# Reading the moving weight columns of a hybrid encoder block from two halves in turn

## The chip, the core and the metric

The kernel runs on one core of a Trainium2 chip. The core has a matrix engine (TensorE, PE in the profile; its weight loads are shown apart as PEld), a vector engine (DVE), a scalar engine (ACT), GpSimd (POOL) and SyncE (SP), which here issues most transfers. All engines work on SBUF; a matmul writes to PSUM. A matmul has two operands: a stationary one of up to 128 x 128, loaded by LDWEIGHTS, and a moving one, whose columns stream past it. The metric is device microseconds for one execution of the whole program. Host work before the launch, such as arranging the weights, is not in it.

## What is computed

One layer of an encoder block for 256 tokens of width 2048: an input projection that feeds two branches (an mLSTM and a gated delta rule, both in two directions), a gated merge of the two, an output projection, and a SwiGLU feed-forward part of width 5632. Cut to the parts that matter here:

```python
h = rms_norm(x, norm_mix_w) * (1 + scale_m) + shift_m
proj = h @ w_in
...
y_a = (jax.nn.sigmoid(a_o.astype(f32)) * h_a).astype(x.dtype) @ w_branch_a
...
y_b = (o_b * jax.nn.silu(b_z.astype(f32))).astype(x.dtype) @ w_branch_b
g_a, g_b = jnp.split(jax.nn.sigmoid(merge), N_BRANCH, axis=-1)
x = x + gate_m * ((g_a * y_a + g_b * y_b) @ w_out)
hf = rms_norm(x, norm_ffn_w) * (1 + scale_f) + shift_f
gt, up = jnp.split(hf @ w_gate_up, 2, axis=-1)
x = x + gate_f * ((jax.nn.silu(gt) * up) @ w_down)
```

Everything is float32. The large products are each computed as three: an operand is split into a high part of type fp32r and the rest, and high x high, low x high and high x low are summed in PSUM.

## The kernel before

There are two kinds of large product. A **product by feature** (`fjob`, lines 173 to 193) gives 128 features for all 256 tokens: the weights are stationary, the activations move, 256 columns at a time (lines 187 to 189). A **product by token** (`tjob`, from line 195) gives 512 features for 128 tokens at a time: the activations are stationary (`xh` and `xl`, the high and the low part, 128 tokens of one block of 128 inputs), and the weights move, 512 columns at a time.

`tjob` gets its weights as chunks of 128 x 4 x 512, 1 MB each, one transfer on SP's queue for one chunk (line 206). ACT copies half a chunk into the high part `wh` (line 209), DVE subtracts that from the raw weights to get `wl` (line 211); both are 128 x 2 x 512. For each of the two blocks in them and each of the two groups of 128 tokens PE issues three products (lines 230 to 232): `xh` with `wh`, `xl` with `wh`, `xh` with `wl`. `wh[:, k]`, the moving operand, is 512 consecutive fp32 values in each partition. The results of both token groups gather in two banks of PSUM, over all inputs, before ACT or DVE takes them out.

These jobs carry the z gate (named `z` in the trace), the values and output gates of the mLSTM (`v`, `o`), both merge gates (`ma`, `mb`), the two branch projections (`ya`, `yb`), the output projection (`o` with `mgh` and `mgl`), the gate and up products of the feed-forward part (`gt`, `up`) and its down product (`d`). The last output projection and the last down product end `by_token`: their last chunk is worked through for one token group after the other, and for the output projection the second group in two pieces of 256 columns (lines 253 to 255).

The work of the two branches between the projections (convolutions, the triangular inverses at lines 684 to 700, scans, small fp32 products such as `ks` at line 630) is threaded between these jobs, so that PE runs a large product while the other engines prepare the next small step. The first stretch, up to about 138 us, is the first input projection in plain fp32 (line 557), while the modulation weights stream in.

On the host, `_groups` cuts a weight matrix into chunks of 512 inputs by 512 outputs, laid out so that a chunk is one contiguous transfer. The gate and up weights are laid out the same way by a reshape of their own (`gu`).

Of the kernel before, what the change touches and what calls it, by code (L numbers as in the profile page):

```python
# [15 lines left out]
P = 128  # L16
# [36 lines left out]
def hybrid_block(ctx: ExitStack, tc: tile.TileContext, xr, nfr, crow, pk_d, cst_d, ada2, ada4, win0, winb, wint, wba, wbb, wo, wgu, wd, out, dbg=None):  # L53
    nc = tc.nc
    V, S, G, PE = nc.vector, nc.scalar, nc.gpsimd, nc.tensor
# [15 lines left out]
    def order(ins, yes=True):  # L71

        return tc.keep_in_program_order(ins) if yes else ins
# [62 lines left out]
    def raw_tile(shape, name):  # L136

        since[0] += 1
        if since[0] > 2 and asked and room[0][0] is st:
            add()  # L140
        return st.tile(shape, F32, tag="raw", bufs=3, name=name)
# [4 lines left out]
    def settle(keep=0, only=None):  # L146

        now = [f for f in behind if only is None or f.__name__ == only]
        for f in now[: len(now) - keep]:
            behind.remove(f)  # L150
            f()
# [13 lines left out]
    def pump():  # L165
        count[0] += 1
        if every[0] and count[0] % every[0] == 0:
            owed[0] += 1
        if owed[0] and not held[0]:
            owed[0] -= 1  # L170
            sums()

    def fjob(name, src, done):
# [5 lines left out]
        for k0 in range(0, KB, 8):  # L179
# [12 lines left out]
                done(o)  # L192
            yield True

    def tjob(name, chunks, xh, xl, done, early=0, by_token=None, steps=1, parts=((0, slice(0, 512)), (1, slice(0, 512)))):

        raws = {}

        def halves(u, k0):
            if u not in raws:
                raws[u] = raw_tile([P, 4, 512], f"raw_{name}_{u}")
                nc.sync.dma_start(raws[u], chunks[u])
            wh = st.tile([P, 2, 512], F32R, tag="wh", bufs=3, name=f"wh_{name}_{u}_{k0}")
            wl = st.tile([P, 2, 512], F32R, tag="wl", bufs=3, name=f"wl_{name}_{u}_{k0}")
            order(S.activation(wh, raws[u][:, k0 : k0 + 2], AF.Copy), early)  # L209
            settle()  # L210
            order(V.tensor_tensor(wl, raws[u][:, k0 : k0 + 2], wh.bitcast(F32), ALU.subtract), early)  # L211
            return wh, wl

        todo = [(u, k0) for u in range(len(chunks)) for k0 in (0, 2)]
        made = []
        for i, q in enumerate(todo[:early]):
            made.append(halves(*q))
            if steps > 1 or i == early - 1:
                yield True
        ps = [acc_ps.tile([P, 512], F32, tag="acc", name=f"acc_{name}_{t}") for t in range(2)]  # L220
        last = 4 * len(chunks) - 1
        if by_token:
            todo = todo[:-2]
        for n, (u, k0) in enumerate(todo):
            wh, wl = made.pop(0) if made else halves(u, k0)
            for k in range(2):
                kk = 4 * u + k0 + k
                for t in range(2):
                    c = slice(t * P, (t + 1) * P)
                    order(PE.matmul(ps[t], xh[:, kk, c], wh[:, k], start=kk == 0, stop=False), early and steps > 1)  # L230
                    PE.matmul(ps[t], xl[:, kk, c], wh[:, k], start=False, stop=False)  # L231
                    PE.matmul(ps[t], xh[:, kk, c], wl[:, k], start=False, stop=kk == last)  # L232
            if k0:
                pump()
                if u == len(chunks) - 1:
                    done(ps)
            yield True
            if early and steps > 1:
                if n + early < len(todo):
                    made.append(halves(*todo[n + early]))  # L240
                yield True
        if by_token:
            w = [halves(len(chunks) - 1, k0) for k0 in (0, 2)]
            by_token()
            for i, (t, part) in enumerate(parts):
                if i > 1:
                    ps.append(acc_ps.tile([P, 512], F32, tag="acc", name=f"acc_{name}_{i}"))
                c = slice(t * P, (t + 1) * P)
                o = ps[i][:, : part.stop - part.start]
                for k in range(4):  # L250
                    kk = last - 3 + k
                    wh, wl = (a[:, k % 2, part] for a in w[k // 2])
                    PE.matmul(o, xh[:, kk, c], wh, start=i == 2 and not k, stop=False)
                    PE.matmul(o, xl[:, kk, c], wh, start=False, stop=False)
                    PE.matmul(o, xh[:, kk, c], wl, start=False, stop=kk == last)
                done(t, ps[i], part)
                yield True
# [734 lines left out]
    last = (0, 1, 2, 1, 2, 2, 1, 1, 3, 0)  # L992
# [433 lines left out]
    for g in range(4):  # L1426
        c = slice(g * 512, (g + 1) * 512)
# [16 lines left out]
def _blocks(w, nb, kb=KB):  # L1444
    k, n = w.shape
    return np.ascontiguousarray(w.reshape(kb, P, nb, P).transpose(2, 1, 0, 3))


def _groups(w):
    k, n = w.shape  # L1450
    return np.ascontiguousarray(w.reshape(k // 512, 4, P, n // 512, 512).transpose(3, 0, 2, 1, 4))


def _fm(v):
    return v.reshape(-1, P).T


def _arrays(x, c, ada_w, ada_b, norm_mix_w, w_in, mlstm_b_i, mlstm_b_f, mlstm_norm_w, gdn_conv_w,
            gdn_A_log, gdn_dt_bias, gdn_norm_w, w_branch_a, w_branch_b, w_out, norm_ffn_w,
            w_gate_up, w_down, norm_final_w):  # L1460
    pk = np.zeros((P, PK_N), np.float32)
    pk[:, PK_ADAB : PK_ADAB + 96] = _fm(ada_b[0])
    pk[:, PK_NMIX : PK_NMIX + 16] = _fm(norm_mix_w[0])
    pk[:, PK_NFFN : PK_NFFN + 16] = _fm(norm_ffn_w[0])
    pk[:, PK_MNW : PK_MNW + 16] = _fm(mlstm_norm_w[0])
    pk[:, PK_GNW : PK_GNW + 16] = _fm(gdn_norm_w[0])
    pk[:, PK_CONV : PK_CONV + 240] = gdn_conv_w[0].reshape(5, 48, P).transpose(2, 1, 0).reshape(P, 240)
    pk[32:64, PK_GB] = gdn_dt_bias[0].reshape(32)
    pk[64:72, PK_GB] = mlstm_b_i[0].reshape(8)
    pk[96:104, PK_GB] = mlstm_b_f[0].reshape(8)  # L1470
    pk[32:64, PK_ALOG] = gdn_A_log[0].reshape(32)

    cst = np.zeros((P, CS_N), np.float32)
    cst[:, CS_ID : CS_ID + P] = np.eye(P)
    r = np.arange(P)
    cst[:, CS_SGN] = np.where(r >= 96, -1.0, 1.0)
    for b in range(4):
        cst[:, CS_OWN + b] = r // 32 == b
        cst[:, CS_NEXT + b] = r // 32 == (b ^ 1)
    for b in range(2):  # L1480
        cst[:, CS_HALF + b] = r // 64 != b
    cst[:, CS_EVEN] = r // 32 % 2 == 0
    cst[:, CS_ODD] = r // 32 % 2 == 1

    w = w_in[0]
    col = lambda o, n=P: np.arange(o, o + n)
    parts = []
    for h in range(NH_B):
        for s in (1, 0, 2):
            parts.append(col(6160 + s * 2048 + h * P))  # L1490
    for h in range(NH_A):
        parts += [col(1024 + h * 256, 256), col(h * 256, 256)]
    gate = np.zeros((D, P), np.float32)
    gate[:, 0:32] = w[:, 14352:14384]
    gate[:, 32:64] = w[:, 14384:14416]
    gate[:, 64:72] = w[:, 6144:6152]
    gate[:, 96:104] = w[:, 6152:6160]
    perm = np.concatenate(parts)
    win = np.concatenate([_blocks(gate, 1), _blocks(w[:, perm], 64)], 0)
    wint = np.concatenate([_groups(w[:, o : o + 2048]) for o in (12304, 2048, 4096, 14416, 16464)], 0)  # L1500
    adaT = ada_w[0].T.reshape(6, KB, P, D)

    bias = np.zeros((2, KB, P, 2), np.float32)
    bias[:, :, :, 0] = ada_b[0].reshape(6, KB, P)[1::-1]
    bias[0, :, :, 1] = 1.0

    gu = w_gate_up[0].reshape(4, 4, P, 2, KD, 512).transpose(4, 3, 0, 2, 1, 5)
    return {
        "xr": np.ascontiguousarray(x[0].reshape(2, P, D).transpose(1, 0, 2)),
        "nfr": np.ascontiguousarray(norm_final_w),  # L1510
        "crow": np.ascontiguousarray(c[0]),
        "pk": pk,
        "cst": cst,
        "ada2": np.ascontiguousarray(np.concatenate([adaT[1::-1], bias], 3).transpose(1, 2, 0, 3)),
        "ada4": np.ascontiguousarray(adaT[2:]),
        "win0": np.ascontiguousarray(win[[*range(13), 49, 50, 51]].transpose(2, 1, 0, 3)),
        "winb": np.ascontiguousarray(win[13:]),
        "wint": wint,
        "wba": _groups(w_branch_a[0]),
        "wbb": _groups(w_branch_b[0]),  # L1520
        "wo": _groups(w_out[0]),
        "wgu": np.ascontiguousarray(gu),
        "wd": _groups(w_down[0]),
    }

# [16 lines left out]
```

## Time and profile before

| what | value |
|---|---|
| time, median of 3 runs | 2053.01 us (2051.42 to 2057.7) |
| span of the profiled execution | 2054.3 us |
| TensorE busy | 2017.2 us (98%) |
| mean granted TensorE clock | 0.992 |
| DVE, ACT busy | 68%, 50% |
| bytes moved | 485.64 MB, 236 GB/s on average |

The profile is one execution on the chip. Its page gives the busy time of each engine, the span in 40 slices with busy shares in tenths, and the chain of work that ended last; it groups instructions by line, with the count behind an x, then the busy time in us, the mean of one in ns, and the idle time of the engine before them. Matmul records overlap, so a record's length is not what a matmul costs: that is the time from one start to the next, read in the timeline. A view of stretches of time gives each engine's busy time in a stretch and the granted clock, for all instructions or those of one line.

### The profile page before, as it was taken

To read this page: it belongs to the slowest core of one execution; us is meant where nothing else is said; L and a number is where in the kernel's file an instruction comes from. 1 tells how busy PE (TensorE), PEld (TensorE's weight loads), DVE (VectorE), ACT (ScalarE), POOL (GpSimd) and SP (SyncE) were. 2 spreads that over 40 slices of the span, in tenths; PEclk is the share of its full clock that TensorE was granted. 3 is DMA by queue.
4 is the path that set the end of the run, shared out by engine and by line. 5 is a ranking of instruction groups with operands and counts; after the bars stand their busy time and mean duration, and the time that the engine had idled before them with its cause. 6 is when DMAs were issued, how large, how long until landed. Compare 5 with 4: busy or idle time off the path is not lost.

```text
span 2054.3 us, 27025 instructions
## 1 busy us (share of the span) xinstructions
PE 2017.2 (98%) x10386; PEld 1698.6 (83%) x10386; DVE 1397.7 (68%) x2062; ACT 1027.4 (50%) x1541; POOL 116.6 (6%) x211
## 2 busy tenths in 40 slices
PE   8999999999999999999999999999999999999998
PEld 6878789988997888889787888788888888878886
DVE  5778877877888788866577778756556554555554
ACT  3146647765675667455534444644444444444443
POOL 0001210111011010100100000200000000000000
PEclk9999999999999999999999999999999999999999
DMA  9986666656666666686776877466666665555553
GB/s 400 420 332 209 195 224 227 220 165 212 226 199 221 245 205 226 205 288 260 260 269 254 309 292 289 163 236 237 237 226 234 254 226 187 193 194 196 193 192 136
DMA packets 78962, 485.64 MB, mean 236 GB/s; under 512 B 10585, under 2 KB 15969, under 8 KB 24433
## 3 DMA queue, kind: packets, MB, share of 16 engines
q1 hardware_dynamic: 63216, 450.69, 60.5%
q0 software_dynamic: 8160, 17.88, 3.9%
q10 hardware_dynamic: 7458, 15.36, 2.0%
q8 instruction: 81, 1.33, 0.3%
q14 instruction: 47, 0.39, 0.1%
HBM read 467.07 MB, written 16.82 MB: 236 GB/s over the span
## 4 chain that ended last, share of the span: by engine, by line
PE 86%; DMA 6%; DVE 5%; ACT 1%; issue 1%; POOL 0%; ACTq 0%; SPq 0%; DVEq 0%; POOLq 0%
PE acc_gt L230 4%; PE acc_gt L232 4%; PE acc_gt L231 4%; PE acc_up L232 4%; PE acc_up L231 4%; PE acc_up L230 4%; PE acc_d L230 4%; PE acc_d L232 4%; PE acc_d L231 4%; DMA ra<-ada 3%; PE acc_o L232 3%; PE acc_o L230 3%; PE acc_o L231 3%; PE acc_b L187 2%; PE acc_b L188 2%; PE acc_b L189 2%
## 5 line engine op out<-in xcount | busy, mean ns | idle before, releaser
L211 DVE TENSOR_TENSOR wl_d<-raw_d,wh_d 128x1024 fp32r<-128x1024 f32 x88 | 107.9, 1226 | 119.9 <-ACT wh_d L209 119.9
L211 DVE TENSOR_TENSOR wl_up<-raw_up,wh_up 128x1024 fp32r<-128x1024 f32 x88 | 107.8, 1226 | 111.9 <-ACT wh_up L209 111.9
L211 DVE TENSOR_TENSOR wl_gt<-raw_gt,wh_gt 128x1024 fp32r<-128x1024 f32 x88 | 108.6, 1234 | 89.1 <-ACT wh_gt L209 89.1
L187 PE MATMUL acc_b<-hh,wh_b 128*128 128x256 f32 x576 | 164.7, 286 | 0.0
L209 ACT ACTIVATE wh_d<-raw_d 128x1024 fp32r<-128x1024 f32 x88 | 93.3, 1061 | 139.0 <-PE acc_d L231 134.0
L189 PE MATMUL acc_b<-hh,wl_b 128*128 128x256 f32 x576 | 160.8, 279 | 0.0
L188 PE MATMUL acc_b<-hl,wh_b 128*128 128x256 f32 x576 | 159.6, 277 | 0.0
L209 ACT ACTIVATE wh_gt<-raw_gt 128x1024 fp32r<-128x1024 f32 x88 | 93.3, 1060 | 128.7 <-PE acc_gt L231 77.3
L111 DVE SCALAR_TENSOR_TENSOR ada<-ada,crow 128x2048 f32<-128x2048 f32 x64 | 146.2, 2284 | 10.8 <-DMA ada<-ada 10.8
L209 ACT ACTIVATE wh_up<-raw_up 128x1024 fp32r<-128x1024 f32 x88 | 93.2, 1060 | 118.0 <-PE acc_up L231 84.2
L230 PE MATMUL acc_gt<-wh_gt,hfh 128*128 128x512 f32 x352 | 139.2, 395 | 0.1
L231 PE MATMUL acc_gt<-wh_gt,hfl 128*128 128x512 f32 x352 | 138.3, 393 | 0.0
L232 PE MATMUL acc_gt<-wl_gt,hfh 128*128 128x512 f32 x352 | 137.5, 391 | 0.0
L230 PE MATMUL acc_up<-wh_up,hfh 128*128 128x512 f32 x352 | 136.9, 389 | 0.0
L231 PE MATMUL acc_up<-wh_up,hfl 128*128 128x512 f32 x352 | 136.9, 389 | 0.0
L232 PE MATMUL acc_up<-wl_up,hfh 128*128 128x512 f32 x352 | 136.9, 389 | 0.0
L230 PE MATMUL acc_d<-wh_d,ffh 128*128 128x512 f32 x344 | 134.3, 391 | 0.0
L231 PE MATMUL acc_d<-wh_d,ffl 128*128 128x512 f32 x344 | 134.3, 390 | 0.0
L232 PE MATMUL acc_d<-wl_d,ffh 128*128 128x512 f32 x344 | 133.9, 389 | 0.0
L557 PE MATMUL first<-x,raw 128*128 128x256 f32 x512 | 115.9, 386 | 6.4 <-ACT x L551 6.4
L557 PEld LDWEIGHTS first<-x,raw 128*128 128x128 f32 x512 | 97.3, 192 | 25.1 <-ACT x L551 12.0
L187 PEld LDWEIGHTS acc_b<-hh,wh_b 128*128 128x128 f32 x576 | 108.4, 188 | 1.2 <-issue 0.9
(374 smaller groups left out, 5262.6 us busy)
## 6 DMA issues: line engine op xcount, KB each, us to landing
ada<-ada SPq DMA_DIRECT2D x64, 1024.0 KB, 4.9
raw_gt<-wgu SPq DMA_DIRECT2D x44, 1024.0 KB, 4.9
raw_up<-wgu SPq DMA_DIRECT2D x44, 1024.0 KB, 4.9
raw_d<-wd SPq DMA_DIRECT2D x44, 1024.0 KB, 4.8
raw_b<-winb SPq DMA_DIRECT2D x36, 1024.0 KB, 5.0
ra<-ada SPq DMA_DIRECT2D x32, 1025.0 KB, 15.3
raw<-win SPq DMA_DIRECT2D x16, 1024.0 KB, 14.5
raw_z<-wint SPq DMA_DIRECT2D x16, 1024.0 KB, 5.5
```

Source lines behind the costliest of these rows:

```text
L111: order(V.scalar_tensor_tensor(raw, raw, 1.0, row_c[:, :D], ALU.mult, ALU.mult, accum_out=mod[:, c : c + 1]), room[0][3] > 1)
L187: PE.matmul(o, wh[:, k], hh[:, kk], start=kk == 0, stop=False)
L188: PE.matmul(o, wh[:, k], hl[:, kk], start=False, stop=False)
L189: PE.matmul(o, wl[:, k], hh[:, kk], start=False, stop=kk == KB - 1)
L209: order(S.activation(wh, raws[u][:, k0 : k0 + 2], AF.Copy), early)
L211: order(V.tensor_tensor(wl, raws[u][:, k0 : k0 + 2], wh.bitcast(F32), ALU.subtract), early)
L230: order(PE.matmul(ps[t], xh[:, kk, c], wh[:, k], start=kk == 0, stop=False), early and steps > 1)
L231: PE.matmul(ps[t], xl[:, kk, c], wh[:, k], start=False, stop=False)
L232: PE.matmul(ps[t], xh[:, kk, c], wl[:, k], start=False, stop=kk == last)
L557: PE.matmul(first[o], raw[:, o], x[:, b], start=b == 0 and o % 2 == 0, stop=b == KB - 1 and o % 2 == 1)
```

## The change

The moving operand of every product by token is read in another order. The 512 columns of a block are taken as two halves of 256, and the read goes column 0 of the first half, column 0 of the second, column 1 of the first, and so on; the two are 256 fp32 values, 1 KB, apart. On the host each run of 512 columns is laid out so that the column which belongs at place 2c + h stands at place c of half h. What PE sees is the columns in their old order, so results land in PSUM as before. The diff, whole:

```diff
+    def woven(a, n=2):
+
+        return a.rearrange("p (h c) -> p c h", h=n)
+
     def tjob(name, chunks, xh, xl, done, early=0, by_token=None, steps=1, parts=((0, slice(0, 512)), (1, slice(0, 512)))):
...
-                    order(PE.matmul(ps[t], xh[:, kk, c], wh[:, k], start=kk == 0, stop=False), early and steps > 1)
-                    PE.matmul(ps[t], xl[:, kk, c], wh[:, k], start=False, stop=False)
-                    PE.matmul(ps[t], xh[:, kk, c], wl[:, k], start=False, stop=kk == last)
+                    order(PE.matmul(ps[t], xh[:, kk, c], woven(wh[:, k]), start=kk == 0, stop=False), early and steps > 1)
+                    PE.matmul(ps[t], xl[:, kk, c], woven(wh[:, k]), start=False, stop=False)
+                    PE.matmul(ps[t], xh[:, kk, c], woven(wl[:, k]), start=False, stop=kk == last)
...
-                    wh, wl = (a[:, k % 2, part] for a in w[k // 2])
+                    wh, wl = (woven(a[:, k % 2])[:, part.start // 2 : part.stop // 2] for a in w[k // 2])
...
+def _woven(w, n=2):
+
+    return np.ascontiguousarray(w.reshape(*w.shape[:-1], -1, n).swapaxes(-1, -2)).reshape(w.shape)
+
+
 def _groups(w):
     k, n = w.shape
-    return np.ascontiguousarray(w.reshape(k // 512, 4, P, n // 512, 512).transpose(3, 0, 2, 1, 4))
+    return _woven(w.reshape(k // 512, 4, P, n // 512, 512).transpose(3, 0, 2, 1, 4))
...
-        "wgu": np.ascontiguousarray(gu),
+        "wgu": _woven(gu),
```

The splits at lines 209 and 211, the transfers, the stationary operands and the products by feature are as they were. In the changed file the three product lines stand at 234 to 236 and those of the token-wise end at 257 to 259.

## The prediction

> **What bounds the kernel now.** Read first, on the profile's page, the busy table, the slices and the chain of work that ended last.
>
> ```profile
> span 2054.3 us, 27025 instructions
> PE 2017.2 (98%) x10386; PEld 1698.6 (83%) x10386; DVE 1397.7 (68%) x2062; ACT 1027.4 (50%) x1541; POOL 116.6 (6%) x211
> ...
> DVE  5778877877888788866577778756556554555554
> ...
> PEclk9999999999999999999999999999999999999999
> ...
> PE 86%; DMA 6%; DVE 5%; ACT 1%; issue 1%; POOL 0%; ACTq 0%; SPq 0%; DVEq 0%; POOLq 0%
> ```
>
> TensorE is idle for 2054.3 − 2017.2 = 37.1 us in all, its clock is fully granted in every slice, and it carries 86% of the chain. Busy records of matmuls overlap, so the table of stretches is read next for a stage that holds only gate and up products, and with it the timeline of one part of it.
>
> ```profile
> 1500.00:1600.00 100.00, 100.00 (x450) 82.39 (x449) 59.80 (x55) 42.32 (x44) 0.00 (x0) 1.00 0.67 242
> ```
>
> ```profile
> 1499.62 0.39 PE L232 MATMUL acc_gt<-wl_gt,hfh 128*128 128x512 f32 x1
> ...
> 1503.93 0.39 PE L230 MATMUL acc_gt<-wh_gt,hfh 128*128 128x512 f32 x1
> ```
>
> In those 100 us (columns: PE, weight loads, DVE, ACT, POOL, clock, DMA share, GB/s) PE never rests, at a clock of 1.00, while DVE has 40% and ACT 58% to spare and the DMA engines a third. One row of the timeline lasts 0.39 us, but the next starts earlier: twenty rows run from 1499.62 to 1503.93, so one product starts every 4.31 / 19 = 226.8 ns. That spacing is the price of a product by token today, 0.443 ns for each moving column. The products by feature move 256 columns; 29 of their rows run like this:
>
> ```profile
> 399.80 0.28 PE L189 MATMUL acc_b<-hh,wl_b 128*128 128x256 f32 x1
> ...
> 402.97 0.28 PE L187 MATMUL acc_b<-hh,wh_b 128*128 128x256 f32 x1
> ```
>
> 3.17 / 28 = 113.2 ns, again 0.442 ns per column. Half the columns take half the time although both load 128 x 128 weights, so neither the weight load nor a fixed cost per instruction sets the pace: the stream of moving columns does. That stream is what the change rewrites.
>
> **The change, part by part.** No instruction, wait, transfer or buffer is added, removed or moved. What differs is the read pattern of the moving operand of these products:
>
> ```profile
> 0.00:2054.00 2054.00, 816.34 (x2064) 389.20 (x2064) 0.99 0.67 236
> ```
>
> ```profile
> L253 PE MATMUL acc_d<-wh_d,ffh 128*128 128x512 f32 x8 | 3.1, 389 | 0.0
> ...
> L253 PE MATMUL acc_o<-wh_o,mgh 128*128 128x256 f32 x8 | 2.3, 282 | 0.0
> L253 PE MATMUL acc_o<-wh_o,mgh 128*128 128x512 f32 x4 | 1.6, 389 | 0.0
> ```
>
> The first row is the table of stretches for line 230 alone: 2064 products; lines 231 and 232 issue as many, and lines 253 to 255 each 8 + 4 of 512 columns and 8 of 256. In units of 512 columns: 3 x 2064 + 3 x 12 + 3 x 8 / 2 = 6240. At 226.8 ns that is 1415 us, 69% of the span. Every nanosecond on one product is 6.24 us on the kernel, because nothing covers PE.
>
> The edits that cost nothing go together. The columns are laid out on the host, outside the timed program; the transfers have the same bytes and contiguous rows; the splits into two halves (L209 and L211) read and write straight as before; the stationary operands and the products by feature keep their patterns. Even if the splits were delayed, the 40% of DVE above covers them.
>
> So one price is unknown: 512 columns read in 256 pairs whose members lie 1 KB apart, where today each column follows its neighbour. No matmul of this trace reads its moving operand other than straight. Bounds from rows, in ns for 512 columns:
>
> ```profile
> 202.63 3.59 PE L630 MATMUL ks<-kq 128*128 128x512 f32 x8
> ```
>
> ```profile
> L630 PE MATMUL ks<-kq 128*128 128x512 f32 x64 | 30.3, 593 | 0.0
> ```
>
> Eight records of full fp32 products, 512 columns each, take 3.59 us, the last one 0.593: (3.59 − 0.593) / 7 = 428.1 ns each, 0.836 ns per column. This is the row in which PE takes moving columns more slowly than in products by token. Its half, 214.1, is less than 226.8. The products by token, which want a new column at each step, are thus 12.7 ns (6%) over twice the speed of the fp32 ones, and that excess grows with the columns, as the 256-column row shows. I read it as a supply of columns that already just fails to keep up. It is an inference, not something that a row shows.
>
> The other reader with gaps between its elements is VectorE:
>
> ```profile
> L698 DVE TENSOR_TENSOR uu<-uu,utmp 64x240 f32<-64x240 f32 x8 | 3.2, 399 | 0.2
> ...
> L698 DVE TENSOR_TENSOR uu<-uu,utmp 64x108 f32<-64x108 f32 x8 | 2.1, 263 | 0.3
> ...
> L698 DVE TENSOR_TENSOR uu<-uu,utmp 64x30 f32<-64x30 f32 x8 | 1.5, 192 | 0.2
> ```
>
> Line 698 takes runs of w elements from rows 32 elements (128 bytes) apart: 240 = 15 x 16, 108 = 27 x 4, 30 = 30 x 1. From 108 to 240 an element costs (399 − 263) / 132 = 1.03 ns. Carried down to 30 that gives 183 ns, and 192 was measured: an element that stands alone costs hardly more, at a pace of one in 1.03 ns. PE wants one in 0.443, which this row doesn't reach.
>
> [...]
>
> The ends: below nothing, the excess goes, 214.1 ns, −12.7 x 6.24 = −79 us. Above, the two columns of a pair no longer come together and PE takes one where it took two. That is 428.1 ns by the fp32 row (+201.3 x 6.24 = +1256 us) or twice today's 226.8 (+1415 us). Still above, VectorE's pace for lone elements: 512 x 1.03 = 527 ns, +1873 us.
>
> I take 428.1: the price is the one that PE itself shows for half its speed, and neighbours that stop being neighbours lose whatever is won by taking them together. A longer product also covers what PE now waits for in these jobs, which the waits of PE list:
>
> ```profile
> PE acc_z L232 <- DVE wl_z L211: 3.0, 2, 2.0
> ...
> PE acc_z L230 <- ACT wh_z L209: 2.5, 1, 2.5
> ...
> PE acc_mb L232 <- DVE wl_mb L211: 1.3, 1, 1.3
> ...
> PE acc_v L232 <- DVE wl_v L211: 0.8, 1, 0.8
> ...
> PE acc_ma L232 <- DVE wl_ma L211: 0.4, 1, 0.4
> ```
>
> That is 8.0 us back. Sum: 2054.3 + 1256 − 8 = 3302 us. The profiled span is 1.3 us over the median of the runs, 2053.0, so the forecast is 3300 us. With 453.6 ns it would be 3460.
>
> **The rivals.**
>
> The excess vanishes, and the kernel is faster. Mechanism: straight reading stumbles once in a while on the place that it has just read, and two places in turn leave each time to recover; the fp32 rows, which take columns at half the pace, show no such excess. Against it: pairs of neighbours are lost. The place is every product by token and the price −79 us: 2053.0 − 79 = 1974 us. It decides if the spacing falls below 226.8. DVE, at 60% in the stage above, would follow; in the early slices of the page it stands at 8 tenths and could keep part of the gain.
>
> No effect: the reads are fetched far enough ahead that order doesn't matter, as VectorE's lone elements suggest. 2053 us. The change would then do as it says and win nothing.
>
> A small loss: each change of place costs a little, say as much again as the excess, +79 us, 2132 us. For it speaks that the spacing already varies with what is read: twelve steps of the value job take 2.75 us, 229 ns each, where the gate job took 226.8.
>
> ```profile
> 199.65 0.39 PE L232 MATMUL acc_v<-wl_v,hh 128*128 128x512 f32 x1
> ...
> 202.40 0.39 PE L232 MATMUL acc_v<-wl_v,hh 128*128 128x512 f32 x1
> ```
>
> A dearer read: if PE, like VectorE, gets one lone element in 1.03 ns, 2053 + 1873 − 8 = 3918 us. Against it: PE already takes a column in 0.443 ns, so its path to the memory is not VectorE's.
>
> **How the numbers follow.** Half speed (428 to 454 ns) 48%; the excess vanishes 32%; no effect 8%; a small loss 5%; dearer than half speed 7%. Slower is 48 + 5 + 7 = 60%, within 0.3% (about 6 us, what a measurement of this kernel can tell from no change) 8%, faster 32%. The forecast's own range is 3270 to 3480 us. As it leaves out half of the chance, the range for the time reaches from a little below the fast case, 1965, to 3480 us; only the dearest read lies outside.
>
> **What would show it.** In the profile after, the spacing of the products by token in the gate stage: near 428 (or 454) ns confirms the step, 214 the fast rival, 227 no effect. The products by feature must stay at 113 ns and the fp32 ones at 428; if they change, it is not the read pattern. With the forecast PE stays near 100% busy, and DVE and ACT fall from 60% and 42% to about half of that in the gate stage, with longer waits of ACT for PE. The forecast is wrong if the spacing of products by token stays under 300 ns.

## The result and the profile after

| | before | after |
|---|---|---|
| time, median | 2053.79 us (4 runs) | 1996.33 us (4 runs) |
| ratio | | 0.9726, 95% interval 0.9707 to 0.9745 |
| span of the profiled execution | 2054.3 us | 1995.8 us |
| TensorE idle | 37.1 us | 48.1 us |

The change makes the kernel 2.7% faster, where the forecast was 61% slower. From the page of the changed kernel:

```profile
span 1995.8 us, 27025 instructions
PE 1947.7 (98%) x10386; PEld 1704.9 (85%) x10386; DVE 1394.1 (70%) x2062; ACT 1023.8 (51%) x1541; POOL 117.9 (6%) x211
...
PEclk9999999999999999999999999999999999999999
```

Instructions, clock and the work of DVE and ACT are as before; PE's busy time fell by 69.5 us, from 2017.2. The timeline of the changed kernel shows why (start in us, length in us, engine, line, product), in 18 rows of a value job, 38 of a product by feature and 18 of a gate job:

```profile
161.06 0.38 PE L236 MATMUL acc_v<-wl_v,hh 128*128 128x512 f32 x1
...
164.73 0.38 PE L235 MATMUL acc_v<-wh_v,hl 128*128 128x512 f32 x1
...
392.73 0.28 PE L189 MATMUL acc_b<-hh,wl_b 128*128 128x256 f32 x1
...
396.92 0.28 PE L187 MATMUL acc_b<-hh,wh_b 128*128 128x256 f32 x1
...
1302.64 0.38 PE L234 MATMUL acc_gt<-wh_gt,hfh 128*128 128x512 f32 x1
...
1306.31 0.38 PE L236 MATMUL acc_gt<-wl_gt,hfh 128*128 128x512 f32 x1
```

In the value and the gate job seventeen steps take 3.67 us: 215.9 ns, where the prediction's rows gave 229 ns for the value job and 226.8 for the gate job. Not only the excess is gone, the difference between the jobs is too. The product by feature stays at 4.19 / 37 = 113.2 ns. 6240 products at 10.9 ns are 68 us, and 2 ns more for the 1920 that read the first activations, as the value job does, make it 72; the time fell by 57.5. Where the rest went is in the table of stretches, cut close to the starts of the first z, branch b, gate and down products. Columns: PE, weight loads, DVE, ACT, POOL, clock, DMA share, GB/s. Before:

```profile
138.00:1012.00 874.00, 858.85 (x5240) 750.35 (x5239) 671.61 (x1277) 541.04 (x954) 101.56 (x192) 0.99 0.66 221
1012.00:1307.00 295.00, 292.14 (x1308) 237.16 (x1306) 217.76 (x266) 130.47 (x170) 2.84 (x5) 0.99 0.75 277
1307.00:1802.00 495.00, 494.94 (x2229) 407.21 (x2228) 288.99 (x277) 221.57 (x245) 9.99 (x6) 1.00 0.62 221
1802.00:2054.00 252.00, 242.55 (x1064) 198.91 (x1062) 125.36 (x134) 103.51 (x115) 0.00 (x0) 0.99 0.53 183
```

After:

```profile
138.00:997.00 859.00, 835.67 (x5238) 751.40 (x5238) 669.89 (x1275) 538.32 (x953) 101.16 (x191) 0.99 0.67 225
997.00:1283.00 286.00, 281.13 (x1310) 238.50 (x1308) 217.76 (x269) 131.22 (x173) 4.14 (x6) 0.99 0.78 286
1283.00:1755.00 472.00, 472.00 (x2228) 410.27 (x2228) 287.77 (x276) 220.27 (x244) 10.31 (x5) 1.00 0.65 232
1755.00:1996.00 241.00, 230.93 (x1061) 199.99 (x1059) 124.55 (x134) 102.86 (x115) 0.00 (x0) 0.98 0.55 191
```

The first input projection, up to 138 us, kept its length. Gate and up gave 23 us and the down products 11: all that their spacing promises (2112 and 1056 products at 11 ns). In the first stretch PE's busy time fell by 23 us, but the stretch shrank by 15 only: PE's idle time there, length less busy, grew from 15.2 to 23.3 us, and in the second from 2.9 to 4.9. What PE waits for there, after:

```profile
PE acc_z L236 <- DVE wl_z L215: 2.9, 3, 1.5
PE acc_mb L236 <- DVE wl_mb L215: 2.7, 2, 1.6
...
PE acc_v L236 <- DVE wl_v L215: 2.4, 3, 1.4
PE acc_ma L236 <- DVE wl_ma L215: 2.1, 1, 2.1
```

These are the low halves of weights that DVE makes. In the rows that the prediction quoted, the low halves of the same four jobs came to 5.5 us; here they come to 10.1. That is 4.6 of the 8 us by which idle time grew in this stretch; the rest is mostly small steps of the branches. DVE is busy 78% of this stretch, and its splits stand in one order with the small steps of the branches.

### The profile page after: what moved, and what is told of

It reads as the page before. It is cut to its first block, busy times and chain, and to the rows that moved or that the text cites. A ratio compares the mean times of both kernels' runs of the same rounds, so it can differ in the third digit from the quotient of the medians.

```text
span 1995.8 us, 27025 instructions
## 1 busy us (share of the span) xinstructions
PE 1947.7 (98%) x10386; PEld 1704.9 (85%) x10386; DVE 1394.1 (70%) x2062; ACT 1023.8 (51%) x1541; POOL 117.9 (6%) x211
## 4 chain that ended last, share of the span: by engine, by line
PE 76%; DMA 9%; DVE 9%; ACT 4%; issue 2%; POOL 0%; ACTq 0%; SPq 0%; DVEq 0%; POOLq 0%
PE acc_gt L234 4%; PE acc_gt L235 4%; PE acc_gt L236 4%; PE acc_up L236 4%; PE acc_up L234 4%; PE acc_up L235 4%; PE acc_d L236 4%; PE acc_d L234 4%; PE acc_d L235 4%; DMA ra<-ada 3%; PE acc_o L236 2%; PE acc_o L234 2%; PE acc_o L235 2%; PE acc_b L187 2%; PE acc_b L189 2%; PE acc_b L188 2%
## 5 line engine op out<-in xcount | busy, mean ns | idle before, releaser
L213 ACT ACTIVATE wh_d<-raw_d 128x1024 fp32r<-128x1024 f32 x88 | 93.0, 1056 | 127.9 <-PE acc_d L235 119.1
```

## Experiments

All runs of read orders share one edit: the read order is chosen by the job's name, and the host lays out each weight to match, so results stay in order.

```diff
+    def woven(a, kind):
...
+        how, n = kind
+        if how == "c":
+            return a.rearrange("p (h c) -> p c h", h=n)
+        if how == "r":
+            return a.rearrange("p (h c r) -> p c h r", h=2, r=n)
+        if how == "n":
+            return a.rearrange("p (b h c) -> p b c h", h=2, c=n)
+        if how == "t":
+            return a.rearrange("p (h c r) -> p r c h", h=2, r=n)
...
+        return a
...
+    i = np.arange(512)
...
+    out[..., i.reshape(-1)] = w
```

Jobs not named read halves in turn, `('c', 2)`, as the change does; `'s'` stands for a straight read and `'og'` for the mLSTM's output gate. Not every run has every one of these orders. The times of these mixed kernels mean nothing; the spacing of each job is the measurement.

### Steps of one length

```diff
+KINDS = {'gt': ('c', 256), 'up': ('c', 128), 'd': ('c', 32), 'yb': ('c', 64), 'ya': ('c', 4), 'z': ('c', 16), 'v': ('c', 8), 'og': ('s', 0)}
```

> One kernel, several read orders, the host layout following each, so that each job's spacing of 512-column products is one measurement. Steps within a read: gate 8 bytes (every second column, then the others), up 16 bytes, branch b 32, down 64, z 128, value 256, branch a 512 (four places in turn), mLSTM output gate straight, the rest halves in turn as in the changed kernel. Theory 'same place': only a read that goes straight on stumbles; every job but the straight one starts a product each 216 ns, the straight one each 227 to 232. [...] Rival 'two places': what helps is to alternate between two places, not to step: 227 ns or more in all stepped jobs, 216 only in the halves.

Time 3008 us. From the timeline of this run, the first and last row of stretches without a break (z, value and gate, up: 20 rows; mLSTM output gate and branch a: 19):

```profile
138.46 0.63 PE L254 MATMUL acc_z<-wh_z,hl 128*128 128x512 f32 x1
...
146.69 0.63 PE L255 MATMUL acc_z<-wl_z,hh 128*128 128x512 f32 x1
...
179.62 0.69 PE L253 MATMUL acc_v<-wh_v,hh 128*128 128x512 f32 x1
...
188.88 0.69 PE L254 MATMUL acc_v<-wh_v,hl 128*128 128x512 f32 x1
...
399.36 0.39 PE L254 MATMUL acc_o<-wh_o,hl 128*128 128x512 f32 x1
...
403.49 0.39 PE L254 MATMUL acc_o<-wh_o,hl 128*128 128x512 f32 x1
...
1356.58 0.45 PE L254 MATMUL acc_ya<-wh_ya,hal 128*128 128x512 f32 x1
...
1361.68 0.45 PE L254 MATMUL acc_ya<-wh_ya,hal 128*128 128x512 f32 x1
...
1595.46 0.69 PE L253 MATMUL acc_gt<-wh_gt,hfh 128*128 128x512 f32 x1
...
1604.10 0.63 PE L254 MATMUL acc_gt<-wh_gt,hfl 128*128 128x512 f32 x1
...
1606.35 0.64 PE L253 MATMUL acc_up<-wh_up,hfh 128*128 128x512 f32 x1
...
1615.12 0.64 PE L254 MATMUL acc_up<-wh_up,hfl 128*128 128x512 f32 x1
```

| step | spacing |
|---|---|
| straight | 4.13 / 18 = 229 ns |
| 8 bytes (gate) | 8.64 / 19 = 455 |
| 16 bytes (up) | 8.77 / 19 = 462 |
| 128 bytes (z) | 8.23 / 19 = 433 |
| 256 bytes (value) | 9.26 / 19 = 487 |
| 512 bytes, four places in turn (branch a) | 5.10 / 18 = 283 |

Steps of 32 and 64 bytes, read in the same way, gave 431 and 433. "Same place" fell: it wanted 216 everywhere. Half speed does exist, 431 to 487 ns, near the 428 that the prediction took from the fp32 products. At 8 bytes the read is nearly as slow as at 16, 455 and 462. "Two places" held in its loose form, 227 or more for every step, without saying how much.

### Runs of neighbours

```diff
+KINDS = {'gt': ('r', 2), 'up': ('r', 4), 'd': ('r', 16), 'yb': ('r', 8), 'ya': ('r', 64), 'ma': ('r', 32), 'mb': ('r', 128)}
```

> Halves in turn as in the change, but with runs of r neighbours from each: gate r = 2, up 4, branch b 8, down 16, gate of branch a 32, branch a 64, gate of branch b 128, the rest r = 1. Theory 'same place': the stumble is paid for each stretch of straight reading of about 16 columns, as the excess of 1 in 16 suggests: 216 ns up to r = 8, between 216 and 227 at 16, back at 227 for 32 and more. Rival 'pattern': any read that is not one plain run escapes it: 216 ns for every r.

Time 2201 us; the timeline of this run, 19 rows each:

```profile
1121.12 0.40 PE L254 MATMUL acc_ya<-wh_ya,hal 128*128 128x512 f32 x1
...
1125.24 0.39 PE L254 MATMUL acc_ya<-wh_ya,hal 128*128 128x512 f32 x1
...
1331.02 0.50 PE L255 MATMUL acc_gt<-wl_gt,hfh 128*128 128x512 f32 x1
...
1336.93 0.51 PE L255 MATMUL acc_gt<-wl_gt,hfh 128*128 128x512 f32 x1
...
1338.50 0.42 PE L254 MATMUL acc_up<-wh_up,hfl 128*128 128x512 f32 x1
...
1343.00 0.42 PE L254 MATMUL acc_up<-wh_up,hfl 128*128 128x512 f32 x1
...
1940.61 0.40 PE L253 MATMUL acc_d<-wh_d,ffh 128*128 128x512 f32 x1
...
1944.93 0.40 PE L253 MATMUL acc_d<-wh_d,ffh 128*128 128x512 f32 x1
```

Runs of 2 take 5.91 / 18 = 328 ns, of 4 250, of 16 240, of 64 229; runs of 8, 32 and 128, read in the same way, gave 243, 237 and 229. Both expectations failed, and in an instructive way: runs of two from two halves keep neighbours together and visit the very same two places in turn as the change does, yet cost 1.5 times as much, 328 ns against 215.9. So it is not enough that two places are at hand; it matters which of the columns comes from which. In the change every column of even place in the order comes from one half and every one of odd place from the other. With runs of two, both come from the same half, and both move together.

### Two places close together

```diff
+KINDS = {'gt': ('n', 4), 'up': ('n', 16), 'd': ('n', 2), 'yb': ('n', 8), 'ya': ('n', 64), 'ma': ('n', 32)}
```

> Two places in turn, but d columns apart instead of 256: down d = 2 (8 bytes), gate 4 (16 bytes), branch b 8, up 16 (64 bytes), gate of branch a 32, branch a 64, the rest 256. Theory 'same place' with a place of about 64 bytes, 16 columns: 216 ns for d of 16 and more, near 227 for d = 2, 4 and 8, where both columns of a pair lie in the same 64 bytes. Rival 'any order but straight': 216 ns for all d. [...]

Time 2010 us; the timeline of this run, 18 rows of the gate job (places 16 bytes apart) and 19 of the down job (8 bytes):

```profile
1303.78 0.38 PE L253 MATMUL acc_gt<-wh_gt,hfh 128*128 128x512 f32 x1
...
1307.44 0.38 PE L255 MATMUL acc_gt<-wl_gt,hfh 128*128 128x512 f32 x1
...
1763.61 0.39 PE L253 MATMUL acc_d<-wh_d,ffh 128*128 128x512 f32 x1
...
1767.72 0.39 PE L253 MATMUL acc_d<-wh_d,ffh 128*128 128x512 f32 x1
```

16 bytes apart: 3.66 / 17 = 215 ns; 8 bytes apart: 4.11 / 18 = 228. Distances of 32 and 64 bytes, read in the same way, gave 215 and 216, and 1 KB gave 215.9 in the changed kernel. Both expectations failed somewhere: "same place" wanted nearly 227 at 4 and 8 columns, "any order but straight" 216 at 2. The border lies between 8 bytes, 228 ns, and 16, 215 ns, not at 64. The distances measured beyond that make no difference.

Together these runs fit one count. Take the columns of even place in the order by themselves, and those of odd place by themselves, and ask how many of four neighbouring columns (16 bytes) each of the two rows takes before it goes on.

| columns of four | orders | spacing |
|---|---|---|
| four | halves in turn; places 16, 32 and 64 bytes apart | 215 to 216 ns |
| two | straight | 227 to 229 |
| two | places 8 bytes apart | 228 |
| two | runs of 4 to 128 | 229 to 250 |
| one | steps of 8 to 256 bytes | 431 to 487 |
| one, and back to the same four after one other column | runs of two; four places in turn | 328; 283 |

The next run keeps the halves 1 KB apart and in turn, and lets each row take two of four columns (gate) or one (up and down). By the spacings in this table the author's estimate was 227 to 255 ns for the gate job and 430 to 490 for the other two.

### Two columns of four, or one

```diff
+KINDS = {'gt': ('t', 2), 'up': ('t', 4), 'd': ('t', 8)}
```

> Halves in turn as in the change, 1 KB apart, but within each half the read takes every second column, then the rest (gate), every fourth (up), every eighth (down). [...] Rival 'recovery', the mechanism of the prediction's fast rival: two places in turn leave each place time to recover; they stay 1 KB apart here, so 216 ns in all three.

Time 2517 us; the timeline of this run, 19 rows of the gate job, 20 each of the up and the down job:

```profile
1304.52 0.40 PE L257 MATMUL acc_gt<-wl_gt,hfh 128*128 128x512 f32 x1
...
1308.61 0.39 PE L257 MATMUL acc_gt<-wl_gt,hfh 128*128 128x512 f32 x1
1309.52 0.61 PE L255 MATMUL acc_up<-wh_up,hfh 128*128 128x512 f32 x1
...
1318.11 0.63 PE L256 MATMUL acc_up<-wh_up,hfl 128*128 128x512 f32 x1
...
2029.33 0.66 PE L257 MATMUL acc_d<-wl_d,ffh 128*128 128x512 f32 x1
...
2038.08 0.66 PE L255 MATMUL acc_d<-wh_d,ffh 128*128 128x512 f32 x1
```

Two columns: 4.09 / 18 = 227 ns. One: 8.59 / 19 = 452 and 8.75 / 19 = 461. All three lie within the estimate, while the two places stayed 1 KB apart and in turn; "recovery", which wanted 216 in all three, is refuted. The runs show which orders are fast and which slow; what in the chip is behind the count they do not show. Nor does the count give the cost of coming back soon: runs of two columns, and four places in turn, take one column at a time, as the steps do, and took 328 and 283 where the steps took 431 to 487. Nor does it give the 13 and 23 ns that runs of 16 and 4 cost over straight reading, or why the steps of 8 to 256 bytes differ among themselves. That stays open.

### Where the missing gain went

```diff
+KINDS = {'z': ('s', 0), 'v': ('s', 0), 'og': ('s', 0), 'ma': ('s', 0), 'mb': ('s', 0), 'yb': ('s', 0), 'ya': ('s', 0), 'o': ('s', 0)}
```

> Halves in turn in gate, up and down products alone; all other products by token straight, with a straight host layout. 3 x 1056 = 3168 products save 227 - 216 = 11 ns each, and PE has no idle time there: 35 us, 2018 us. Theory 'cover': the part of the gain that is missing in the changed kernel (58 of 73 us) was lost in the earlier stages, where weights and small steps come too late for a faster PE, so here all of the 35 us shows. Rival 'spread': every product gains less than its spacing says, also here, 35 x 58 / 73 = 28 us, 2026 us.

2020.46 us, ratio 0.9839 (0.9823 to 0.9855) of a kernel before at 2052.55 on that chip. By the interval 30 to 36 us are saved, which holds the 35 of "cover" and leaves "spread", 28, just outside.

```diff
+KINDS = {'gt': ('s', 0), 'up': ('s', 0), 'd': ('s', 0)}
```

> Halves in turn in all products by token but gate, up and down; those straight. The complement of the run with gate, up and down alone. 6240 - 3168 = 3072 products, most of them at 229 before, save 11 to 13 ns: 37 us by their spacing. Theory 'cover': PE waits more for late weight halves and small steps in these stages, and 24 to 28 us are left, 2025 to 2029 us. Rival: the loss comes only when both parts are changed, so 33 us or more here, 2020 us or less.

2027.27 us, ratio 0.9868 (0.9845 to 0.989), 23 to 32 us of the 37 that the spacing promises, 27 in the middle: "cover" again. The two parts, 33 and 27, add up to the gain of the whole within their intervals, so the loss is not one of both together. It sits in the stages with the small steps, as the stretches showed. From the first z to the first branch b product (first row this run, second row the run with gate, up and down alone):

```profile
138.00:996.00 858.00, 833.56 (x5236) 749.86 (x5235) 669.83 (x1275) 537.81 (x953) 100.63 (x190) 0.99 0.67 225
138.00:1012.00 874.00, 857.37 (x5237) 749.20 (x5237) 670.86 (x1275) 540.73 (x953) 101.29 (x191) 0.99 0.66 221
```

PE is idle there for 24.4 us in this run and for 16.6 where these jobs read straight; in the whole change it was 23.3, before it 15.2. Late low halves are part of what PE waits for; that they are the whole of the loss was not tried by itself.

### Products by feature too

```diff
+    def tok_mix(a):
+        return a.rearrange("p (h c) -> p c h", h=2)
+
+    def tok_back(a):
+        return a.rearrange("p (c h) -> p h c", h=2)
+
+    def tok_rows(a):
+        return a.rearrange("p (h c) -> p h c", h=2)
...
-                PE.matmul(o, wh[:, k], hh[:, kk], start=kk == 0, stop=False)
+                PE.matmul(o, wh[:, k], tok_mix(hh[:, kk]), start=kk == 0, stop=False)
...
-            S.activation(ev, ps, AF.Copy)
+            S.activation(tok_rows(ev), tok_back(ps), AF.Copy)
```

> The changed kernel, and the products by feature read their 256 tokens from two halves of 128 in turn as well; their results then stand in PSUM with tokens of the two halves alternating, and ACT takes them out with a step of two. Theory 'same place': 2352 products of 256 columns fall from 113 to 108 ns, 12 us, of which these threaded stages let through two thirds or all: 8 to 12 us under the changed kernel, 0.962 to 0.968 of the kernel before. Rival: ACT takes twice the time for PSUM read with a step (374 ns more on 36 + 13 evictions, 18 us of ACT, on the way of the next small steps): no gain or a loss against the changed kernel, 0.972 or more.

> The changed kernel itself, beside the run with both kinds, on the same chip. All theories: 0.972 of the kernel before, products by feature at 113 ns.

With both kinds: 1993.03 us, ratio 0.9709 (0.9688 to 0.973). The changed kernel beside it: 1995.5 us, 0.9715 (0.9697 to 0.9734). The two can't be told apart, and the 0.962 to 0.968 of "same place" lie outside the interval. The timeline of the run with both kinds, 16 rows of a product by feature:

```profile
399.81 0.28 PE L198 MATMUL acc_b<-hh,wl_b 128*128 128x256 f32 x1
...
401.48 0.27 PE L198 MATMUL acc_b<-hh,wl_b 128*128 128x256 f32 x1
```

1.67 / 15 = 111 ns, from 113; half of 215.9 would be 108. In the changed kernel the 256-column pieces that end the output projection, read from two places too, have the same pace (24 rows):

```profile
1275.34 0.27 PE L257 MATMUL acc_o<-wh_o,mgh 128*128 128x256 f32 x1
...
1277.90 0.28 PE L259 MATMUL acc_o<-wl_o,mgh 128*128 128x256 f32 x1
```

2.56 / 23 = 111 ns as well. What sets the pace at this length no run shows. The group table of the run with both kinds shows that taking results out of PSUM with a step of two costs ACT nothing:

```profile
L369 ACT ACTIVATE pad<-acc_b 128x256 f32<-128x256 f32 x36 | 13.5, 375 | 3.6 <-PE acc_b L198 3.4
```

375 ns, as in the changed kernel, whose row for the same work is:

```profile
L333 ACT ACTIVATE pad<-acc_b 128x256 f32<-128x256 f32 x36 | 13.5, 375 | 3.2 <-PE acc_b L189 3.0
```

So the expected 12 us were at most 2352 x 2 ns = 5 us, and what is left of that is below what these runs can tell. The rival of this run, ACT at twice the time, fell with these two rows.

## Why the prediction was wrong

**What bounds the kernel** held in the main: another order of the moving columns, and nothing else, took a product of the gate job from 226.8 to 215.9 ns, and the count of products was right. "Nothing covers PE" held for the gate, up and down products, where every nanosecond came through; in the stretch of the first jobs about a third of what PE saved came back as waiting, so that over the whole kernel 1 ns on a product was worth 5 us and not 6.24 (the 72 us of the spacings are 11.5 ns on each of 6240 products, and 57.5 us came of them). That no fixed cost sets the pace of a product fits the straight reads, 226.8 ns for 512 columns and 113.2 for 256; from two places 256 columns took 111, where half of 215.9 is 108.

**The step that failed** is the one that priced the pairs: "the two columns of a pair no longer come together and PE takes one where it took two". It put 428.1 ns, +1256 us, where the runs show 215.9 ns for each product, −69.5 us of PE's busy time and −57.5 us on the kernel. That neighbours are fetched together was read out of the 6% by which products by token take longer than half of an fp32 product. That the excess is a supply that just fails to keep up was the author's inference, and no run shows a supply by itself. The runs of read orders show that two neighbours in a row are not what a fast read needs: 215 to 216 ns go with orders whose even and odd places each take four neighbouring columns one after the other, and straight reading, with two of four, takes 227 to 229. The change goes from two to four. Half speed, taken as the price, is real, 431 to 487 ns, but it belongs to orders that take one of four (the runs with steps, and with every fourth and eighth column of the halves).

**The row that was misread** is the fp32 one. It showed 428.1 ns for 512 columns, and so that 226.8 is 6% over its half. The prediction drew from this that the supply has no room, and so that any disorder must cost. But the row says nothing of orders other than straight. That both ends were open was stated in the prediction, and the choice between them had no row.

**The fast rival** had the sign and nearly the size for a product, 226.8 to 215.9 ns where it took 214.1, by the mechanism that places recover in turn. The run with every second, fourth and eighth column refuted that: 227, 452 and 461 ns. On the kernel it gave 1974 us; 1996 came out. Of those 22 us, 11 are PE's larger idle time, 48.1 against 37.1 us. Another 9.5 are the smaller fall of its busy time, 69.5 us where the rival had 79. By the spacings that would be 7: 1.8 ns on 6240 products, 11 us, less the 4 that the first jobs saved beyond 10.9 ns. That its size came so close is luck, as its mechanism did not hold. That DVE could keep part of the gain in the early stages was said, without a price.

**No effect** was held up by VectorE's lone elements. The row was read too kindly: 192 against 183 ns is 9 ns on 30 elements, 0.3 each, a third of the 1.03 that an element costs in longer runs, and not "hardly more". PE's own lone columns cost 431 to 487 ns for 512 (0.84 to 0.95 ns each), a little less than VectorE's 1.03: the row was no reason for a free read, and the dearer read priced from it was still too dear.

The signs that were named to watch read clearly. The spacing is 215.9, far under the 300 named as the border. The products by feature stay at 113, and eight fp32 products take 3.60 us, where they took 3.59. PE is still at 98%. In the gate and up stretch DVE went from 58% to 61% and ACT from 45% to 47%, instead of to half.

## What to carry to other kernels

Where fp32r products follow each other, read their start-to-start spacing and divide it by the columns; if 512 columns take about 227 ns instead of 216, as here, try an order that takes even columns from one place and odd ones from another: with the two places 16, 32 or 64 bytes or 1 KB apart it gave the 5% back in these runs. The fast orders here were those whose even and odd places each took four neighbouring columns one after the other; a plain step, even one of 8 bytes, took 431 to 487 ns, about twice the time. Before pricing a gain per product over the whole kernel, split the kernel by who feeds PE: here the feed-forward stages, where PE's waits did not grow, gave all of it, and the early stages, with a busy DVE and small steps, about two thirds (15 of 23 us).

## What was not expected of the hardware

Two reads that touch the same places in turn, single columns or runs of two, took 216 and 328 ns. Steps of 8 bytes and of 16 cost nearly the same, 455 and 462; 32 to 128 bytes are a little cheaper (431 to 433), 256 bytes dearer (487). Straight reads varied by stage, 229 ns in the value job and 227 in the gate job, and reads from two places did not (215.9 in both). A step of two in PSUM cost ACT nothing, 375 ns with it and without.
